# Part of a modulation's products moved to TensorE, its last two chunks singly, and another PSUM bank for what follows

## The chip, the cores and the metric

The kernel runs on one core of one Trainium2 chip. The metric is the device time of one execution in microseconds (us). Engines are named as the profile names them: PE is TensorE (its weight loads are PEld), DVE is VectorE, ACT is ScalarE, POOL is GpSimd, SP is SyncE, which issues most DMAs.

## The reference, cut to what matters

The program computes three transformer-like blocks on 512 tokens of width 1024. The change touches only the start of the first block. There the input `x` is modulated by a vector that comes from the conditioning input `c`, and the result is multiplied by a wide weight:

```python
mod = silu(c) @ w_ada + b_ada                 # w_ada: 1024 x 3072
shift, scale, gate = split(mod, 3)            # the first two are needed before anything else
h = x * (1 + scale) + shift                   # 512 x 1024
p = h @ w_in                                  # 1024 x 3712; the branches read slices of p
...
x = layer_norm(ALPHA * x + gate * o)          # the scaled x is kept until here
```

Everything is float32. For `h @ w_in` each float32 operand is split into a high and a low part and three products are added (high by high, high by low, low by high).

## The kernel before, in words

The width of 1024 is worked on in eight chunks of 128, numbered k = 0 to 7. The modulation phase (the `with self.ordered():` block in `block1`) streams `w_ada`, `x` and `w_in` from DRAM, and for each chunk does this:

1. Modulation: shift and scale of the chunk are dot products of silu(c) (tile `sc`, 128 x 8) with 128 columns of `w_ada`. `ada_acc` (called by `part`) lets ACT form the first of eight scaled terms and DVE add the other seven into the tile `acc`, a term for each 128 rows of `w_ada`. That leaves 128 partial sums a column, one for each partition; `sums` adds them on PE by a product of `acc` with a vector of ones, 128 x 1, and DVE adds the bias into `mod`.
2. `turned_x`: PE transposes the chunk of `x` by four 128 x 128 transposes.
3. `modulated`: ACT forms h from the transposed x with scale and shift, ACT rounds it to the high part (`aH`), DVE takes the low part (`aL`), and ACT writes the scaled x (`xa`, tiles named `res`).
4. `wsplit`: ACT and DVE split the chunk's row of `w_in` into `wh` and `wl`.
5. PE multiplies: 8 products with `aH` into four banks `psv`, 4 into two banks `psw` and `psk`, then 6 with `aL`.

Chunks are loaded in units (`UNITS`: first chunk, number of chunks): 0, 1, then pairs. A pair's modulation is found for both chunks at once; its accumulation is in two halves of 512 rows of `w_ada` (`part(cur, 0)`, `part(cur, 1)`). PE's order is fixed by a token, so a product stands where the source issues it: the `sums` of the next unit stand behind the eight `psv` products of a unit's last chunk, and the remaining ten products of that chunk behind them. DMAs are issued by SP in source order as well; the raw rows of `w_in` have three slots, so the load for chunk k waits for DVE's split of chunk k - 3.

After chunk 7, `psums` closes the banks and opens four new rings, which take up the eight banks in the order of its list. The first thing PE does then is `r_gemm(0)`, 24 products of 128 x 512 into the ring `po`, then `k_gemm(1)` into `mm`. Before, `po` is the last bank, the one in which `psk` lies; `psk` is read out by `shift_evac`, an ACT and a DVE instruction (`k<-sm,omu,sh`).

The lines that matter are short:

```python
def part(cur, q):
    ada_acc(cur[2], cur[1][q], range(4 * q, 4 * q + 4), 4 * q, self.act)
...
self.mm(pa[:, n * j + i : n * j + i + 1], cur[2][:, j, i * P : (i + 1) * P], self.ones[:, 0:1])
...
self.psums([("mm", 2), ("mg", 2), ("sm", 3), ("po", 1)])
```

Of the kernel before, what the change touches and what calls it, by code (L numbers as in the profile page):

```python
# [20 lines left out]
P = 128  # L21
T = 512
D = 1024
# [12 lines left out]
BEGUN = 1  # L36
LOW = 3
EARLY = 3
UNITS = ((0, 1), (1, 1), (2, 2), (4, 2), (6, 2))
TT = ("sm", "sm", "mm", "mm")  # L40
NFILL = 69
ORDER = "r0 A0 k1 g0 k2 r1 g0 n0 r2 f11 g0 f1 t0 g1 m0 g1 k3 g1 g2 l0 g2 r3 g3 l1 g2 f5 l2 f2 g3 l3 f3 l4 f2 g3 l5 f3 l6 f3 l7"
# [20 lines left out]
class Kern:  # L63
# [90 lines left out]
    def f(self, ap):  # L154
        return ap.bitcast(F32)
# [146 lines left out]
    def block1(self):  # L302
        nc, I, tc = self.nc, self.I, self.tc
        w_in, w_ada = I["w_in"], I["w_ada"]
# [9 lines left out]
        sc = b([P, 8], "sc")  # L314
# [8 lines left out]
        xaD = self.dp.tile([8, P, T], F32, tag="xaD", name="xaD")  # L323

        hH = [self.tl(self.ap_, [P, T], "aH", F32R) for _ in range(8)]
        hL = [self.tl(self.ap_, [P, T], "aL", F32R) for _ in range(8)]
# [14 lines left out]
        def ada_acc(acc, raw, steps, q0=0, first=None):  # L341

            for q in steps:
                if q == 0 and first:
                    first(acc, raw[:, q - q0], AF.Copy, scale=sc[:, q : q + 1])
                elif q == 0:
                    self.ts(acc, raw[:, q - q0], sc[:, q : q + 1])
                else:
                    self.stt(acc, raw[:, q - q0], sc[:, q : q + 1], acc, ALU.mult, ALU.add)
# [7 lines left out]
        xa = [self.tl(self.rp, [P, T], f"res{k}") for k in range(8)]  # L357

        def load(u):

            k0, n = UNITS[u]
            cs = slice(k0 * P, (k0 + n) * P)
            ada = []
            for q in range(n):
                raw = self.tl(sp, [P, 16 * P], "ada", bufs=5).rearrange("p (q j m) -> p q j m", j=2, m=n * P)
                r0, r1 = (0, D) if n == 1 else (512 * q, 512 * q + 512)
                for j in range(2):
                    src = w_ada[r0:r1, j * D + cs.start : j * D + cs.stop]
                    self.st(nc.sync.dma_start(out=raw[:, :, j, :], in_=src.rearrange("(k p) m -> p k m", p=P)))
                ada += [raw] if n == 2 else [raw[:, 0:4], raw[:, 4:8]]  # L370
                if q == 0:
                    xt = self.tl(sp, [P, NB, 2 * P], "xt", bufs=3)[:, :, : n * P]
                    self.st(nc.sync.dma_start(out=xt, in_=xv[:, :, cs]))
            return xt, ada, self.tl(sp, [P, 2, 2 * P], "acc")[:, :, : n * P]

        def wrows(k):
            ks = slice(k * P, (k + 1) * P)
            raw = self.wraw()
            rv = raw[:, : 6 * P].rearrange("p (k m) -> p k m", k=1)
            for o, c0, n in ((0, 512, T), (T, 3584, P), (T + P, 2048, P)):  # L380
                self.st(nc.sync.dma_start(out=rv[:, 0, o : o + n], in_=w_in[ks, c0 : c0 + n]))
            return rv

        def part(cur, q):
            ada_acc(cur[2], cur[1][q], range(4 * q, 4 * q + 4), 4 * q, self.act)

        def sums(u, cur):

            k0, n = UNITS[u]
            m2 = lambda z: z[:, 0:16].rearrange("p (j k) -> p j k", j=2)[:, :, k0 : k0 + n]  # L390
            pa = self.ptl("sm")
            for j in range(2):
                for i in range(n):
                    self.mm(pa[:, n * j + i : n * j + i + 1], cur[2][:, j, i * P : (i + 1) * P], self.ones[:, 0:1])
            self.tt(m2(mod), pa[:, 0 : 2 * n].rearrange("p (j k) -> p j k", j=2), m2(bada1), ALU.add)

        def turned_x(i, xt):
            ps = self.ptl("sm")
            for tb in range(NB):
                self.turn(ps[:, tb * P : (tb + 1) * P], xt[:, tb, i * P : (i + 1) * P])  # L400
            return ps
# [9 lines left out]
        with self.ordered():  # L411
            self.petoken = "start"
            cur = load(0)
            rv = wrows(0)
            pt = turned_x(0, cur[0])
            part(cur, 0)
            part(cur, 1)
            sums(0, cur)
            w_ = self.wsplit(rv, 1, 6 * P)
            modulated(0, pt)  # L420
            for k in range(8):
                wh, wl = w_
                u = [k in range(k0, k0 + n) for k0, n in UNITS].index(True)
                k0, n = UNITS[u]
                new, end = k == k0 and k0 + n < 8, k == k0 + n - 1
                if k < 7 and n == 2:
                    rv = wrows(k + 1)
                if new:
                    nxt = load(u + 1)
                if k < 7 and n == 1:  # L430
                    rv = wrows(k + 1)
                for f in loads[3 * k : 3 * k + 3]:
                    f()
                tok = [slice(tb * P, (tb + 1) * P) for tb in range(NB)]
                if new:
                    part(nxt, 0)
                    if n == 1:
                        part(nxt, 1)
                for tb in range(NB):
                    self.mm(psv[tb], hH[k][:, tok[tb]], wh[:, 0, :T], k == 0, False)  # L440
                    self.mm(psv[tb], hH[k][:, tok[tb]], wl[:, 0, :T], False, False)
                    if tb == (3 if end else 0) and k < 7:
                        pt = turned_x(0 if end else 1, (nxt if end else cur)[0])
                        if end:
                            sums(u + 1, nxt)
                            cur = nxt
                        w_ = self.wsplit(rv, 1, 6 * P)
                        modulated(k + 1, pt)
                        if new and n == 2:
                            part(nxt, 1)  # L450
                oz = ((T, psw), (T + P, psk))
                for o, pz in oz:
                    self.mm(pz, wh[:, 0, o : o + P], hH[k], k == 0, False)
                    self.mm(pz, wl[:, 0, o : o + P], hH[k], False, False)
                for tb in range(NB):
                    self.mm(psv[tb], hL[k][:, tok[tb]], wh[:, 0, :T], False, k == 7)
                for o, pz in oz:
                    self.mm(pz, wh[:, 0, o : o + P], hL[k], False, k == 7)
            self.petoken = None
            for k in range(8):  # L460
                self.st(nc.gpsimd.dma_start(out=xaD[k], in_=xa[k]))
        for _, turn in late:
            turn()
        sx.close()
# [142 lines left out]
        for tb in range(NB):  # L607
            vgs.append(a_([P, 8, 64], f"vn{tb}"))
            self.act(vgs[tb], psv[tb].rearrange("p (h i) -> p h i", i=64), AF.Gelu_apprx_tanh)
        self.psums([("mm", 2), ("mg", 2), ("sm", 3), ("po", 1)])  # L610

        def a_load():
            bsp = a_([P, 4, P], "bsp")
# [22 lines left out]
        def a_norm(tb):  # L636
            vg = vgs[tb]
            w = self.tl(av, [P, 8, 4], "lw", bufs=2)
            nc.vector.tensor_reduce(out=w[:, :, 0], in_=vg, axis=AX.X, op=ALU.add)
            self.ts(w[:, :, 0], w[:, :, 0], 1.0 / 64)  # L640
            self.tt(vg, vg, w[:, :, 0:1].to_broadcast([P, 8, 64]), ALU.subtract)
            sq = self.tl(av, [P, 8, 64], "gsq", bufs=1)
            self.act(sq, vg, AF.Square)
            nc.vector.tensor_reduce(out=w[:, :, 1], in_=sq, axis=AX.X, op=ALU.add)
            self.ts(w[:, :, 2], w[:, :, 1], 1.0 / 64, LN_EPS)
            self.pow_(w[:, :, 3], w[:, :, 2], -0.5)
            self.tt(vg, vg, w[:, :, 3:4].to_broadcast([P, 8, 64]), ALU.mult)
            return vg.rearrange("p h i -> p (h i)")
# [102 lines left out]
        for op, p in ORDER:  # L751
            if op == "r":
                r_gemm(p)
            elif op == "k":
                k_gemm(p)
            elif op == "g":
                go(p)
            elif op == "l":
                lmat(p // 2, p % 2)
            elif op == "f":  # L760
                fill(p)
            elif op == "A":
                bsp, wsp = a_load()
            elif op == "n":
                vn = [a_norm(tb) for tb in range(NB)]
            elif op == "t":
                wmT = a_turn(wsp, bsp)
            elif op == "m":
                for j in range(4):
                    a_mix(j, vn, bsp, wmT)  # L770
                a_free()
# [7 lines left out]
        r = lambda s, n, dt=F32: rp.tile(s, dt, tag=n, name=n)  # L779
# [226 lines left out]
        for c in range(NC_R):  # L1006
            late = [posts.pop(0) for _ in range(LATE[c])]
            steps = chain(c, between(c + 1, late))
            while True:
                with first():  # L1010
                    i = next(steps, None)
# [30 lines left out]
        o = Acts(oc)  # L1042
# [808 lines left out]
```

## Time and profile before

| | us |
|---|---|
| median of 3 runs (lowest to highest) | 1600.42 (1599.26 to 1603.02) |
| the profiled execution | 1600.12 |
| its span from first to last instruction | 1598.1 |
| PE busy in the span | 1531.5 (96%) |
| DVE busy | 915.0 (57%) |
| ACT busy | 722.9 (45%) |
| POOL busy | 256.7 (16%) |

All times inside the trace are counted from the span's start. The modulation phase takes the first 64.6 us. A float32 product that is not in the rounded form (the sums with ones, the transposes of other tiles) runs as two records on PE, so the trace counts two where the source has one. The granted clock (PEclk) is given as a share of 2.4 GHz: 1.00, or 0.50 for 1.2 GHz. Up to 18.4 us the trace holds no record of the clock and the column shows 1.00.

### The profile page before, as it was taken

How to read it: one execution, taken by the hardware profiler on the slowest of the kernel's cores; microseconds unless marked ns; L12 is line 12 of the kernel's file. 1: busy time of each engine (PE TensorE's matmuls, PEld its weight loads, DVE VectorE, ACT ScalarE, POOL GpSimd, SP SyncE). 2: the span in 40 equal slices, each digit the busy share in tenths (PEclk: the TensorE clock that was granted, in tenths of full speed). 3: DMA queues.
4: the chain of work that ended last, by engine and by line, in shares of the span. 5: the costliest groups of instructions: out<-in, count | busy, mean ns of one | idle time of the engine just before them, and what ended most of it. 6: DMA issues, size and time to landing. Idle time of an engine off the chain costs nothing.

```text
span 1598.1 us, 21745 instructions
## 1 busy us (share of the span) xinstructions
PE 1531.5 (96%) x8261; PEld 1298.2 (81%) x8261; DVE 915.0 (57%) x1621; ACT 722.9 (45%) x1318; POOL 256.7 (16%) x418
## 2 busy tenths in 40 slices
PE   5899989989999999999999999999999999999997
PEld 4787768889878899888888888888888988888886
DVE  6767677668767748233343456667755714343445
ACT  3545326646656556232232335667645524332231
POOL 3212110324300032000000033223323200000000
PEclk9999999999999999999999999999999999999999
DMA  9632556532233133333333232322213224232421
GB/s 312 190 104 85 104 150 174 171 109 77 60 79 86 41 93 93 94 102 94 93 94 104 79 106 60 109 70 76 71 53 106 93 66 120 81 103 66 132 79 53
DMA packets 260828, 161.16 MB, mean 101 GB/s; under 512 B 29553, under 2 KB 241124, under 8 KB 260724
## 3 DMA queue, kind: packets, MB, share of 16 engines
q1 hardware_dynamic: 258036, 153.40, 33.5%
q0 software_dynamic: 2544, 6.11, 1.3%
q8 instruction: 65, 1.06, 0.3%
q14 instruction: 39, 0.32, 0.1%
q10 hardware_dynamic: 144, 0.26, 0.0%
HBM read 146.90 MB, written 11.53 MB: 99 GB/s over the span
## 4 chain that ended last, share of the span: by engine, by line
PE 67%; DVE 5%; issue 2%; ACT 1%; DMA 1%; SPq 0%; POOL 0%; DVEq 0%; POOLq 0%; ACTq 0%
PE mm L144 58%; PE sm L144 4%; PE po L144 1%; PE sc L144 1%; DMA sw<-tr 1%; DVE bL L134 1%; DVE wl L124 1%; DVE res L124 1%; SPq L1320 0%; PE sm L150 0%; DVE mlom L134 0%; DVE hgmm L134 0%; PE pt L1380 0%; PE kv L144 0%; DVE mlpy L124 0%
## 5 line engine op out<-in xcount | busy, mean ns | idle before, releaser
L124 DVE TENSOR_TENSOR wl<-raw,wh 128x1024 fp32r<-128x1024 f32 (+3 forms) x244 | 287.1, 1178 | 294.4 <-ACT wh L141 290.3
L141 ACT CAST wh<-raw 128x1024 fp32r<-128x1024 f32 (+3 forms) x244 | 241.9, 994 | 459.6 <-PE mm L144 365.3
L144 PE MATMUL mm<-bL,wh 128*128 128x512 f32 (+1 forms) x752 | 280.3, 376 | 0.7 <-DVE bL L134 0.7
L144 PE MATMUL mm<-bH,wl 128*128 128x512 f32 (+1 forms) x752 | 279.7, 375 | 0.0
L144 PE MATMUL mm<-bH,wh 128*128 128x512 f32 (+1 forms) x752 | 278.3, 377 | 0.7 <-ACT t L138 0.7
L144 PE MATMUL mm<-aH,wh 128*128 128x512 f32 (+1 forms) x656 | 239.1, 366 | 5.0 <-ACT gsh L138 2.3
L144 PE MATMUL mm<-aL,wh 128*128 128x512 f32 (+1 forms) x656 | 236.7, 362 | 0.0
L144 PE MATMUL mm<-aH,wl 128*128 128x512 f32 (+1 forms) x656 | 236.2, 362 | 0.0
L144 PEld LDWEIGHTS mm<-bL,wh 128*128 128x128 f32 x752 | 140.7, 188 | 27.8 <-DVE bL L134 1.1
L144 PEld LDWEIGHTS mm<-bH,wl 128*128 128x128 f32 x752 | 140.8, 188 | 26.9
L144 PEld LDWEIGHTS mm<-bH,wh 128*128 128x128 f32 x752 | 139.0, 188 | 28.6 <-ACT t L138 1.1
L144 PEld LDWEIGHTS mm<-aH,wh 128*128 128x128 f32 x656 | 124.4, 190 | 26.0 <-ACT gsh L138 2.7
L144 PEld LDWEIGHTS mm<-aH,wl 128*128 128x128 f32 x656 | 124.6, 190 | 19.0 <-issue 0.2
L144 PEld LDWEIGHTS mm<-aL,wh 128*128 128x128 f32 x656 | 124.8, 190 | 17.7 <-issue 0.4
L144 PE MATMUL mm<-wh,aH 128*128 128x512 f32 x288 | 113.2, 395 | 1.7 <-ACT aH L141 1.7
L144 PE MATMUL mm<-wl,aH 128*128 128x512 f32 x288 | 112.9, 394 | 0.0
L144 PE MATMUL mm<-wh,aL 128*128 128x512 f32 x288 | 108.8, 393 | 0.0
L141 ACT CAST aH<-t 128x512 fp32r<-128x512 f32 (+1 forms) x74 | 40.9, 563 | 75.6 <-DVE t L124 75.5
L124 DVE TENSOR_TENSOR aL<-t,aH 128x512 fp32r<-128x512 f32 (+1 forms) x74 | 45.0, 617 | 36.8 <-ACT aH L141 36.8
L144 PEld LDWEIGHTS mm<-wh,aH 128*128 128x128 f32 x288 | 54.8, 190 | 13.0 <-ACT aH L141 1.8
L144 PEld LDWEIGHTS mm<-wl,aH 128*128 128x128 f32 x288 | 54.8, 190 | 11.4
L144 PEld LDWEIGHTS mm<-wh,aL 128*128 128x128 f32 x288 | 54.5, 190 | 11.6
(552 smaller groups left out, 2612.6 us busy)
## 6 DMA issues: line engine op xcount, KB each, us to landing
raw<-in_mlp_w_dram SPq DMA_DIRECT2D x128, 512.0 KB
raw<-in_hgrn_w_in_dram SPq DMA_DIRECT2D x32, 512.0 KB
raw<-in_w_in_dram SPq DMA_DIRECT2D x23, 512.0 KB
ada<-in_w_ada_dram SPq DMA_DIRECT2D x16, 512.0 KB
raw<-in_w_out_dram SPq DMA_DIRECT2D x10, 512.0 KB
raw<-in_w_ada_dram SPq DMA_DIRECT2D x8, 512.0 KB
raw<-in_mla_w_o_dram SPq DMA_DIRECT2D x8, 512.0 KB
raw<-in_hgrn_w_o_dram SPq DMA_DIRECT2D x8, 512.0 KB
```

The source lines that it names most:

```text
L124: self.st((eng or self.nc.vector).tensor_tensor(out=out, in0=a, in1=b, op=op))
L134: self.st(self.nc.vector.scalar_tensor_tensor(out=out, in0=a, scalar=s, in1=b, op0=op0, op1=op1))
L141: self.st(self.nc.scalar.copy(out=out, in_=in_))
L144: i = self.nc.tensor.matmul(out, l, r, start=start, stop=stop, **kw)
```

## The change

Five things change.

1. `direct(u)`: for unit 0 all eight terms of the modulation, and for the units of two chunks the second four, are no longer accumulated on DVE. `sums` multiplies the loaded blocks of `w_ada` (as weights) with the column of `sc` on PE and adds them in PSUM, behind the product of `acc` with ones where there is one. Unit 0 has 16 products instead of 2, the units of two chunks 20 instead of 4 each; DVE loses 7, 4 and 4 accumulations and ACT one.
2. `UNITS`: chunks 6 and 7 are units of their own. Each has 7 accumulations of 128 x 256 on DVE, and its own sums.
3. `load`: the units of one chunk, but for unit 0, load `w_ada` in four DMAs of 256 KB in place of two of 512 KB.
4. In a chunk, the two products of `aL` for `psw` and `psk` stand ahead of the four for `psv`.
5. `psums` lists `po` ahead of `sm`, so `po` is now the bank in which the parameter tile `pb` was transposed, and `psk`'s bank belongs to `sm`. The stores of `xa` to DRAM are issued in the source behind `a_norm` and without the token. In the built program they stand on POOL's queue where they stood before, one for one.

```diff
-UNITS = ((0, 1), (1, 1), (2, 2), (4, 2), (6, 2))
+UNITS = ((0, 1), (1, 1), (2, 2), (4, 2), (6, 1), (7, 1))
...
-                r0, r1 = (0, D) if n == 1 else (512 * q, 512 * q + 512)
...
+                rows = ((0, D),) if u == 0 else ((0, 512), (512, D)) if n == 1 else ((512 * q, 512 * q + 512),)
+                for r0, r1 in rows:
+                    q0 = 0 if n == 2 else r0 // P
...
-        def part(cur, q):
-            ada_acc(cur[2], cur[1][q], range(4 * q, 4 * q + 4), 4 * q, self.act)
+        def parts(u, cur):
+            for q in range(2):
+                if 4 * q not in direct(u):
+                    ada_acc(cur[2], cur[1][q], range(4 * q, 4 * q + 4), 4 * q, self.act)
+
+        def direct(u):
+
+            return range(8) if u == 0 else range(4, 8) if UNITS[u][1] == 2 else ()
...
-                    self.mm(pa[:, n * j + i : n * j + i + 1], cur[2][:, j, i * P : (i + 1) * P], self.ones[:, 0:1])
+                    m = slice(i * P, (i + 1) * P)
+                    steps = [(cur[2][:, j, m], self.ones[:, 0:1])] if u else []
+                    steps += [(cur[1][q // 4][:, q % 4, j, m], sc[:, q : q + 1]) for q in direct(u)]
+                    for o, (l, r) in enumerate(steps):
+                        self.mm(pa[:, n * j + i : n * j + i + 1], l, r, o == 0, o == len(steps) - 1)
...
+                for o, pz in oz:
+                    self.mm(pz, wh[:, 0, o : o + P], hL[k], False, k == 7)
                 for tb in range(NB):
                     self.mm(psv[tb], hL[k][:, tok[tb]], wh[:, 0, :T], False, k == 7)
-                for o, pz in oz:
-                    self.mm(pz, wh[:, 0, o : o + P], hL[k], False, k == 7)
             self.petoken = None
-            for k in range(8):
-                self.st(nc.gpsimd.dma_start(out=xaD[k], in_=xa[k]))
...
-        self.psums([("mm", 2), ("mg", 2), ("sm", 3), ("po", 1)])
+        self.psums([("mm", 2), ("mg", 2), ("po", 1), ("sm", 3)])
```

On PE the program begins, before, with the transposes of chunk 0 (`xt`), the two products of `acc` with ones, and then the first products of `h`:

```order
L150 MATMUL sm_179<-ident,xt_172 128x128 x4
L144 MATMUL sm_192<-ones,acc_174 128x1 x2
L144 MATMUL mm_153<-wh_196,aH_122 128x512
L144 MATMUL mm_153<-wl_197,aH_122 128x512
L144 MATMUL mm_154<-wh_196,aH_122 128x512
```

In the changed program the same place reads:

```order
L150 MATMUL sm_179<-ident,xt_172 128x128 x4
L144 MATMUL sm_184<-sc,ada_169 128x1 x16
L144 MATMUL mm_153<-wh_202,aH_122 128x512
L144 MATMUL mm_153<-wl_203,aH_122 128x512
L144 MATMUL mm_154<-wh_202,aH_122 128x512
```

Sixteen products on the loaded `w_ada` itself stand where two on the accumulated tile stood, ahead of every product of `h`.

On PE at the end of chunk 1's `psv` products, before, the transposes of chunk 2 and the four sums of unit 2 (chunks 2 and 3) stand ahead of chunk 1's other products:

```order
L150 MATMUL sm_294<-ident,xt_265 128x128 x4
L144 MATMUL sm_299<-ones,acc_270 128x1 x4
L144 MATMUL sm_157<-aH_123,wh_243 128x512
L144 MATMUL sm_157<-aH_123,wl_244 128x512
L144 MATMUL sm_158<-aH_123,wh_243 128x512
```

In the changed program:

```order
L150 MATMUL sm_298<-ident,xt_273 128x128 x4
L144 MATMUL sm_303<-ones,acc_278 128x1
L144 MATMUL sm_303<-sc,ada_275 128x1 x4
L144 MATMUL sm_303<-ones,acc_278 128x1
L144 MATMUL sm_303<-sc,ada_275 128x1 x4
L144 MATMUL sm_303<-ones,acc_278 128x1
L144 MATMUL sm_303<-sc,ada_275 128x1 x4
L144 MATMUL sm_303<-ones,acc_278 128x1
L144 MATMUL sm_303<-sc,ada_275 128x1 x4
L144 MATMUL sm_157<-aH_123,wh_251 128x512
```

Twenty sums stand there now, each group opened by one that needs DVE's `acc`; the same row stands at the end of chunk 3 for unit 3.

On DVE around chunk 7 of the changed program (`aL_136` is chunk 6's low part, `aL_137` chunk 7's, `wl_592` chunk 7's weight and `wl_713` that of `r_gemm(0)`):

```order
L124 TENSOR_TENSOR aL_136<-h_95_539,aH_128 128x512
L134 SCALAR_TENSOR_TENSOR acc_561<-ada_554,sc,acc_561 128x2x128 x7
L124 TENSOR_TENSOR mod<-sm_587,bada_111 128x2
L124 TENSOR_TENSOR wl_592<-raw_562,wh_591 128x768
L124 TENSOR_TENSOR wl_713<-raw_710,wh_712 128x1024
L124 TENSOR_TENSOR aL_137<-h_104_595,aH_129 128x512
```

Before, it reads:

```order
L124 TENSOR_TENSOR aL_136<-h_96_510,aH_128 128x512
L124 TENSOR_TENSOR wl_537<-raw_525,wh_536 128x768
L124 TENSOR_TENSOR wl_672<-raw_669,wh_671 128x1024
L124 TENSOR_TENSOR aL_137<-h_101_540,aH_129 128x512
L294 COPY pb<-sm_587 128x69
```

An accumulation of seven and a `mod` now stand between chunk 6's low part and chunk 7's weight.

## Rows read from the trace of the kernel before

**Rows 1.** The page's first line.
```profile
span 1598.1 us, 21745 instructions
```
**Rows 2.** Stretches: busy time and records of each engine, granted clock, DMA share.
```profile
core 0: us, PE busy (x) PEld busy (x) DVE busy (x) ACT busy (x) POOL busy (x), PEclk, DMA share, GB/s
...
24.50:28.30 3.80, 0.02 (x1) 0.05 (x1) 3.49 (x5) 0.83 (x1) 0.00 (x0) 1.00 1.08 361
...
29.60:35.50 5.90, 5.90 (x17) 4.63 (x18) 4.72 (x7) 3.22 (x5) 0.55 (x1) 0.50 1.10 351
35.50:64.60 29.10, 28.58 (x142) 23.36 (x140) 19.50 (x33) 17.14 (x26) 7.25 (x18) 1.00 0.81 250
64.60:69.30 4.70, 0.05 (x1) 0.00 (x0) 4.70 (x10) 4.09 (x8) 0.72 (x3) 1.00 1.06 257
69.30:73.10 3.80, 3.75 (x9) 2.93 (x10) 2.55 (x4) 0.63 (x1) 1.81 (x2) 0.55 0.73 192
73.10:120.00 46.90, 46.66 (x272) 37.96 (x271) 30.71 (x48) 21.26 (x32) 9.61 (x6) 1.00 0.29 90
...
148.20:155.00 6.80, 5.91 (x17) 4.59 (x17) 4.95 (x9) 2.94 (x5) 3.27 (x3) 0.50 0.44 116
```
**Rows 3.** Timeline, chunks 0 and 1: start, duration, engine, line, operation [idle before <-releaser].
```profile
8.57 1.12 PE L150 MATMUL sm<-ident,xt 128*128 128x128 f32 x4 [5.35 <-DMA xt<-in_x_dram]
...
11.93 1.02 PE L144 MATMUL sm<-ones,acc 128*128 128x1 f32 x4 [2.24 <-DVE acc L134]
...
12.38 0.57 PE L144 MATMUL sm<-ones,acc 128*128 128x1 f32 x2
...
12.98 0.16 DVE L124 TENSOR_TENSOR mod<-sm,bada 128x2 f32<-128x2 f32 x1 [1.11 <-PE sm L144]
...
14.66 0.80 PE L144 MATMUL mm<-wh,aH 128*128 128x512 f32 x1 [1.71 <-ACT aH L141]
...
15.53 3.65 DVE L134 SCALAR_TENSOR_TENSOR acc<-ada,sc,acc 128x256 f32<-128x256 f32 x7 [0.20 <-ACT acc L138]
...
19.24 0.61 PE L144 MATMUL sm<-ones,acc 128*128 128x1 f32 x4 [0.28 <-DVE acc L134]
```
**Rows 4.** Timeline, the sums of unit 2 and the first product of chunk 2.
```profile
22.66 5.48 DVE L134 SCALAR_TENSOR_TENSOR acc<-ada,sc,acc 128x512 f32<-128x512 f32 x7 [0.41 <-ACT acc L138]
...
28.28 1.44 PE L144 MATMUL sm<-ones,acc 128*128 128x1 f32 x8 [3.78 <-DVE acc L134]
...
33.99 0.63 PE L144 MATMUL mm<-wh,aH 128*128 128x512 f32 x1
```
**Rows 5.** Timeline, the last unit's second half on DVE and its sums on PE.
```profile
49.03 3.11 DVE L134 SCALAR_TENSOR_TENSOR acc<-ada,sc,acc 128x512 f32<-128x512 f32 x4
...
52.28 1.02 PE L144 MATMUL sm<-ones,acc 128*128 128x1 f32 x8 [0.52 <-DVE acc L134]
...
52.28 0.91 PE L144 MATMUL sm<-ones,acc 128*128 128x1 f32 x7 [0.52 <-DVE acc L134]
```
**Rows 6.** What engines waited for ahead of instructions on `acc`: us in total, times.
```profile
  DMA ada<-in_w_ada_dram: 4.0, 1
```
**Rows 7.** Timeline, the first products behind the phase, on PE, and what releases them.
```profile
68.56 0.74 DVE L134 SCALAR_TENSOR_TENSOR k<-sm,omu,sh 128x512 f32<-128x512 f32 x1
...
69.35 0.53 PE L144 MATMUL po<-aH,wh 128*128 128x512 f32 x1 [4.70 <-DVE k L134]
...
73.10 0.39 PE L144 MATMUL po<-aH,wh 128*128 128x512 f32 x1
...
76.55 0.39 PE L144 MATMUL mm<-aH,wh 128*128 128x512 f32 x1
```
**Rows 8.** Timeline of PE ahead of a later fall of the clock.
```profile
144.71 0.95 PE L144 MATMUL po<-ind,cum 128*128 128x2 f32 x8
145.59 1.16 PE L144 MATMUL sm<-AR,BK 64*128 64x128 f32 x8
149.09 2.07 PE L144 MATMUL sm<-AR,BK 64*128 64x128 f32 x8 [2.34 <-ACT res L141]
```

More of the change, by code (lines that the diff above doesn't have):

```diff
@@ L365, in load @@
                 raw = self.tl(sp, [P, 16 * P], "ada", bufs=5).rearrange("p (q j m) -> p q j m", j=2, m=n * P)
-                r0, r1 = (0, D) if n == 1 else (512 * q, 512 * q + 512)
-                for j in range(2):
-                    src = w_ada[r0:r1, j * D + cs.start : j * D + cs.stop]
-                    self.st(nc.sync.dma_start(out=raw[:, :, j, :], in_=src.rearrange("(k p) m -> p k m", p=P)))
+                rows = ((0, D),) if u == 0 else ((0, 512), (512, D)) if n == 1 else ((512 * q, 512 * q + 512),)
+                for r0, r1 in rows:
+                    q0 = 0 if n == 2 else r0 // P
+                    for j in range(2):
+                        src = w_ada[r0:r1, j * D + cs.start : j * D + cs.stop]
+                        dst = raw[:, q0 : q0 + (r1 - r0) // P, j, :]
+                        self.st(nc.sync.dma_start(out=dst, in_=src.rearrange("(k p) m -> p k m", p=P)))
                 ada += [raw] if n == 2 else [raw[:, 0:4], raw[:, 4:8]]
@@ L415, in block1 @@
             pt = turned_x(0, cur[0])
-            part(cur, 0)
-            part(cur, 1)
             sums(0, cur)
@@ L434, in block1 @@
                 tok = [slice(tb * P, (tb + 1) * P) for tb in range(NB)]
[L435 to L438, printed above, removed]
+                if new and n == 1:
+                    parts(u + 1, nxt)
                 for tb in range(NB):
@@ L449, in block1 @@
                         if new and n == 2:
-                            part(nxt, 1)
+                            parts(u + 1, nxt)
                 oz = ((T, psw), (T + P, psk))
@@ L765, in block1 @@
                 vn = [a_norm(tb) for tb in range(NB)]
+                for k in range(8):
+                    nc.gpsimd.dma_start(out=xaD[k], in_=xa[k])
             elif op == "t":
```

## The prediction

> **What bounds the kernel now.** I read the page first, then the table of stretches, then the timeline of the first 80 us, then the view of the tile `acc`. The reader is to see three things.
>
> PE sets the end of the modulation phase and of what follows. From 35.5 to 64.6 it is busy 28.58 of 29.10 us, from 73.1 to 120 it is busy 46.66 of 46.90 [rows 2]. So what is added to PE's work there is paid in full, and only PE's idle stretches can be won back.
>
> There are three of these worth naming: 2.24 us before the first sums, which wait for DVE's accumulation [rows 3]; 3.78 us before the sums of unit 2, for the same reason [rows 4]; and 4.70 us after the phase, when the first `po` product waits until DVE has read `psk` out of the same bank, at 68.56 + 0.74 [rows 7].
>
> The clock makes two of them dearer. Behind the second and the third idle stretch the granted clock is 0.50 (29.60 to 35.50, and most of 69.30 to 73.10) [rows 2]. Nine `po` products take 69.35 to 73.10, 0.42 us each; the next fifteen take 73.10 to 76.55, 0.23 each [rows 7].
>
> w_ada's transfers are no bound: over the whole phase an engine sat idle for them once, 4.0 us before the first accumulation [rows 6].
>
> **The change part by part.** First the price of a sum. A 128 x 1 product is two records. At 1.00 seven records take 0.91 us and eight 1.02 [rows 5], so a record is 0.11. In the first burst the last two of four start 0.45 after the first (12.38 against 11.93) [rows 3], so there a record is 0.22; that is the lower clock, whatever the column shows so early.
>
> (a) Unit 0. The accumulation goes (2.24 us of PE's wait), but PE gets 32 records for 4. They can start when the four transposes are through, at about 9.5 (8.57 + 1.12, less the 0.2 by which products overlap) [rows 3]. At 0.22 they end at 9.5 + 7.0 + 0.2 = 16.7; before, the sums ended at 12.95. Loss 3.7 us. Were they to run at 0.11 they would end at 13.2, a loss of 0.2. I take 3.7: the engine has done nothing but four transposes, and the four sums at this place did run at 0.22.
>
> Chunk 1 hangs on the same chain: from `mod` at 12.98 to its sums at 19.24 it is 6.3 us of h, high part, scaled x and DVE's 3.65 [rows 3], which the change leaves alone. So it comes 3.7 later too, and PE reaches the sums of unit 2 at 24.50 + 3.7 = 28.2 [rows 2].
>
> (b) Unit 2. DVE now has three of the seven accumulations, 5.48 x 3/7 = 2.35, and is done at 22.66 + 3.7 + 2.35 = 28.7 [rows 4]. The sums start at 28.8, against 28.28: the idle time that the edit removes has been spent by (a). There are 40 records for 8. At 0.11 they end at 33.3, against 29.72. The ten products between them and chunk 2 took 29.72 to 33.99 at the lower clock, 4.3 us; at 1.00 they take 2.3, so chunk 2 begins at 35.6, 1.6 late, and saves another 0.7 because before it ran at 0.50 until 35.50. Loss by chunk 2's end 0.9, if the clock holds.
>
> (c) Unit 3. Before, these sums did not wait [no idle between 35.5 and 64.6 beyond 0.52, rows 2, 5]. 32 more records at 0.11: 3.5 us.
>
> (d) Units 4 and 5, chunks 6 and 7 singly. The first has 4 records for 8 (gain 0.45) and its seven accumulations, 3.65, are ready about 0.4 sooner than the half that was waited for 0.52 [rows 3, 5]: gain 0.8. The second has 4 records (loss 0.45), and its chain from `mod` is again 6.3 us, for which PE has 18 products of 0.23 and four transposes at half of the first ones' 1.12, 4.7 us. PE waits 1.6. Loss 2.1. The smaller pieces of w_ada are hidden: they were not waited for, and PE is later than before. Without that cover the four extra issues on SP would cost up to their own time; SP's next load waits for a slot of raw weights anyway.
>
> (e) The bank. `po` waits for the read of `pb`, made while chunk 7 multiplies. So the 4.70 us go, and with them the fall of the clock behind: 9 x (0.42 - 0.23) = 1.7. Gain 6.4. What is late next is the weight of `k_gemm(1)`, a row that DVE does before the phase ends, and then nothing for 24 products each. The stretch from 73.1 shows that DVE is busy 30.71 of 46.90 us, so it can follow when PE is 6.4 nearer.
>
> (f) Two `aL` products earlier: same products, other order, 0. The stores of scaled x: same places on POOL's queue, 0 from both sides.
>
> (g) The clock in the bursts. This is the only unknown of size. Two bursts, (b) and (c), last 4.4 us each and hold nothing but 128 x 1 products. No burst before is longer than 1.44. The nearest rows speak against their holding the clock. At 28.28 PE began with 1.44 us of sums, went on with dense products, and got no higher clock until 35.50, 7.2 us; at 69.35 it began with dense products and had it after 3.75 [rows 2, 4, 7]. And at 148.2 the clock fell behind 2.0 us of small products (eight of 128 x 2, eight on half the rows) and 2.34 of idling [rows 8], less idle time than in the other cases. So I take it that the clock falls behind a burst of sums as it did behind idling, and that each burst brings one stretch at 0.50 like those at 29.6 (5.9 us and more) and 148.2 (6.8 us) [rows 2]. 6.8 us at half the clock are 3.4 us lost. Bounds for each: 0, and 3.4.
>
> The Trainium skill, TensorE: Matmul & The Clock Gate, section "Why this matters for your kernels", blames idle gaps between bursts of matmuls for the loss of the clock. By that rule two bursts in which PE is never idle would keep 1.00, and the sum would be 6.8 us lower; rows 8 agree with it only in part.
>
> Sum for the phase: (a, b) 0.9, (c) 3.5, (d) -0.8 + 2.1, together 5.7; with two falls 12.5. Less 6.4 for the bank: 6.1 us slower. The profiled execution is 1600.12 (span 1598.1 [rows 1] and 2.0 around it), which is 0.3 under the median. 1606.2, and I say 1606. Behind 120 us every engine's order is the one before, so I let the shift run through to the end.
>
> **The rivals.**
>
> Only one burst costs the clock (the other straddles dense work on both sides): 6.1 - 3.4 = 2.7, 1602.8. For it: falls came at differing delays after the work stopped. Against it: both bursts are three times the longest seen.
>
> The clock holds in both: 6.1 - 6.8 = -0.7, 1599.4. For it: PE is never idle. Against it: the two places named in (g).
>
> The other side, faster: sums keep the clock as dense products do, and it rises in the first burst already. At 69.35 it rose 3.75 us after PE began; counted from the transposes at 8.57 it would rise at 12.3. By then 13 records are done, the other 19 take 2.1, and the sums end at 14.6, 1.6 late instead of 3.7. With the clock held later, -0.7 - 2.1 = -2.8, 1597.3. It decides where a stretch of sums at 9.5 goes from 0.22 to 0.11 a record. Against it: the stretch from 28.28, where sums and dense products together did not raise the clock for 7.2 us. With bounds of 0.2 in (a) it reaches 1596.
>
> A loss further on: PE comes 6.4 us nearer to DVE and ACT behind the phase, meets a wait there, and the bank's gain goes: up to 12.5, 1612. Against it: DVE's and ACT's idle time from 73.1 to 120 (16 and 26 us) [rows 2].
>
> That the change does not do what it says holds for the stores alone, and costs nothing.
>
> **How the numbers follow.** Two falls 0.48 (its own range 1603.5 to 1609: falls of 2.7 to 4.5 each as they come early or late in a burst, and (a) at 3.0 to 3.7), one fall 0.12, the clock holds 0.16, it rises early 0.19, a loss further on 0.05. The range reaches from 1596.5, the early rise's lower part, to 1609.5; outside are the dearest case and the edges. A measurement here can tell about 0.2%, 3.2 us. Slower by more: 0.45 + 0.04 + 0.05 = 0.54. Within: 0.03 of the first, 0.08, 0.14 and 0.05: 0.30. Faster by more, below 1597.2: 0.02 of the third and 0.14 of the fourth, 0.16.
>
> **What would show it.** In the changed profile: 32 sum records from about 9.5, at 0.22 each, and `mod` near 16.7; sums of unit 2 from about 28.8, with a clock of 0.50 during or behind them and records that go from 0.11 to 0.22 on the way; the same behind chunk 3; a wait of about 1.6 us for `acc` before the sums of chunk 7; the phase's end near 77 rather than 64.6; and the first `po` product right behind it, without idle time and at 0.23 us. If the clock stays at 1.00 from 20 to 77, or the first burst speeds up on its way, the forecast is wrong by the terms given. If the first `po` product still waits, (e) is wrong.

## The result, and the profile after

Five runs of the changed kernel have the median 1612.95 us (1608.11 to 1614.86), five of the kernel before 1599.81. The ratio is 1.0071 (95% interval 1.0059 to 1.0083): 11.4 us slower, 9 to 13 by the interval. The forecast was 1606, its range ended at 1609.5. The direction came true, the size did not.

The profiled execution took 1611.48, its span is 1609.2 for 1598.1 [rows 1]: 11.1 more. Three stretches add up to that. They meet at two places that both traces have: the start of the first `po` product less its wait, which I call the phase end, and the second group of the small products `po<-ind,cum` (128 x 2; eight records a group), which stands about 50 us behind it.

| stretch | before | after | difference | forecast |
|---|---|---|---|---|
| start to phase end | 64.65 | 78.51 | +13.9 | +12.5 |
| phase end to second group of `ind` | 52.62 | 50.05 | -2.6 | -6.4 |
| from there to the end of the span | 1480.8 | 1480.6 | -0.2 | 0 |

The first step came as forecast. Timeline of PE and DVE in the changed kernel (start, duration, engine, line, operation, count, [idle before <- releaser]):

```profile
9.40 6.83 PE L144 MATMUL sm<-sc,ada 128*128 128x1 f32 x32
...
16.26 0.16 DVE L124 TENSOR_TENSOR mod<-sm,bada 128x2 f32<-128x2 f32 x1 [12.02 <-PE sm L144]
...
28.77 0.35 PE L144 MATMUL sm<-ones,acc 128*128 128x1 f32 x2 [0.63 <-DVE acc L134]
28.98 1.03 PE L144 MATMUL sm<-sc,ada 128*128 128x1 f32 x8
...
30.10 1.83 PE L144 MATMUL sm<-sc,ada 128*128 128x1 f32 x8
...
36.06 0.77 PE L144 MATMUL sm<-aH,wh 128*128 128x512 f32 x1
```

The 32 records of unit 0 run at 0.21 each and `mod` is there at 16.26 for 12.98 [rows 3]. Unit 2's records begin at 28.77 (forecast 28.8); eight take 1.03, and from 30.10 on eight take 1.83: the price nearly doubles in the middle of the burst, as term (g) said. The stretches show the clock (us, busy time and records of PE, PEld, DVE, ACT, POOL, granted clock, DMA share, GB/s):

```profile
30.13:40.37 10.24, 10.24 (x39) 9.37 (x40) 2.77 (x4) 2.61 (x4) 0.55 (x1) 0.50 0.59 192
40.37:50.61 10.24, 10.24 (x66) 9.03 (x66) 2.95 (x4) 3.23 (x5) 0.54 (x1) 1.00 1.10 310
50.61:57.44 6.83, 6.83 (x23) 5.77 (x23) 2.77 (x4) 2.61 (x4) 0.54 (x1) 0.50 0.53 146
57.44:78.50 21.06, 19.18 (x94) 15.59 (x93) 14.44 (x31) 10.88 (x17) 4.96 (x13) 1.00 0.43 125
78.50:102.90 24.40, 24.34 (x109) 19.03 (x107) 20.43 (x35) 17.73 (x27) 8.27 (x11) 1.00 0.62 153
102.90:104.62 1.72, 0.00 (x1) 0.00 (x1) 1.72 (x5) 1.00 (x2) 0.00 (x0) 1.00 0.07 19
104.62:108.64 4.02, 4.02 (x11) 3.15 (x12) 2.48 (x5) 0.00 (x0) 3.85 (x2) 0.58 0.78 216
```

In the first and the third row PE is busy all the time, and the clock is 0.50: two falls, one for each burst, at 1.2 of 2.4 GHz. Ahead of the first burst PE stood 0.63 for DVE; in e2 below, both falls come without any such wait. The last two rows are what the forecast did not have. PE works almost without a gap from the phase's end to 102.90 (24.34 of 24.40 us), stands for 1.72, and goes on at half clock from 105.2 to 108.6. The chain behind that wait, in the timeline of all engines:

```profile
78.51 0.40 PE L144 MATMUL po<-aH,wh 128*128 128x512 f32 x1
...
80.42 0.38 SPq L624 DMA_DIRECT2D wsp<-in_w_spatial_dram  x1
...
88.21 1.09 POOL L625 TENSOR_SCALAR_AFFINE_SELECT wsp<-wsp 128x1024 f32<-128x1024 f32 x1 [7.18 <-DMA wsp<-in_w_spatial_dram]
89.28 3.32 POOL L246 TENSOR_TENSOR lw<-lw,pwm 128x8 f32<-128x8 f32 x2
...
90.99 0.69 DVE L124 TENSOR_TENSOR vn<-vn,lw 128x512 f32<-128x512 f32 x1 [2.28 <-POOL lw L246]
...
103.82 0.74 DVE L134 SCALAR_TENSOR_TENSOR k<-mm,omu,sh 128x512 f32<-128x512 f32 x1
...
104.62 0.50 PE L144 MATMUL mm<-aH,wh 128*128 128x512 f32 x1 [1.72 <-DVE k L134]
```

Read it from below. PE waits for a bank of `mm` that DVE has yet to read; it does so at 103.82 (`k_gemm`'s shift). DVE is late, since from 90.99 on it does row after row without idling and before that it stood 2.28 us for POOL. POOL makes the powers of `a_norm` (`lw<-lw,pwm`), and these stand in its queue behind the masking of `w_spatial`, which waits 7.18 us for its load. The first `po` product, with 4.70 of wait in [rows 7], has none any more. The same chain lies in the kernel before, under PE's wait and its half clock, where it cost nothing (timeline of the kernel before):

```profile
71.29 1.09 POOL L618 TENSOR_SCALAR_AFFINE_SELECT wsp<-wsp 128x1024 f32<-128x1024 f32 x1 [5.52 <-DMA wsp<-in_w_spatial_dram]
...
74.07 0.69 DVE L124 TENSOR_TENSOR vn<-vn,lw 128x512 f32<-128x512 f32 x1 [1.66 <-POOL lw L246]
...
92.08 0.74 DVE L134 SCALAR_TENSOR_TENSOR k<-mm,omu,sh 128x512 f32<-128x512 f32 x1
...
94.99 0.48 PE L144 MATMUL mm<-aH,wh 128*128 128x512 f32 x1
```

DVE was through at 92.82 and PE came at 94.99: a slack of 2.2 us. In the changed kernel, counted from the phase end, PE would have come to this place at 24.4 us for 30.3, 6.0 sooner, and DVE was through at 26.1 for 28.2, 2.1 sooner. 6.0 less the slack and less what DVE gained is 1.7, the wait that the trace shows. With half of the 3.4 us at half clock behind it that makes 3.4 of the 3.8 us that are missing in the table.

### The profile page after: what moved, and what is told of

Its sections match the earlier page's. It is cut to its first block, busy times and chain, and to the rows that moved or that the text cites. A ratio compares the mean times of both kernels' runs of the same rounds, so it can differ in the third digit from the quotient of the medians.

```text
span 1609.2 us, 21933 instructions
## 1 busy us (share of the span) xinstructions
PE 1551.3 (96%) x8353; PEld 1317.8 (82%) x8353; DVE 908.0 (56%) x1614; ACT 723.1 (45%) x1318; POOL 255.9 (16%) x418
## 4 chain that ended last, share of the span: by engine, by line
PE 69%; DVE 4%; issue 2%; ACT 1%; POOL 1%; DMA 0%; SPq 0%; DVEq 0%; POOLq 0%; ACTq 0%
PE mm L144 59%; PE sm L144 5%; PE po L144 2%; PE sc L144 1%; DVE bL L134 1%; DVE res L124 1%; DVE wl L124 1%; PE pt L1389 0%; PE sm L150 0%; DVE hgmm L134 0%; DVE mlom L134 0%; PE kv L144 0%; DVE mlpy L124 0%; PE po L150 0%; DVE mlpy L134 0%
## 5 line engine op out<-in xcount | busy, mean ns | idle before, releaser
L144 PEld LDWEIGHTS mm<-wh,aL 128*128 128x128 f32 x288 | 55.2, 192 | 11.8
```

Of the source, the lines that this page charges most:

```text
L144: i = self.nc.tensor.matmul(out, l, r, start=start, stop=stop, **kw)
```

## The experiments

Two theories stood against each other for the missing 3.8 us. P: POOL's wait for `w_spatial`, by the chain above. D: DVE simply has too much to do behind the phase. A third question was what the products on TensorE cost, and whether their bursts cost the clock. Each row below is one kernel: the ratio to the kernel before, then from its profile the phase end, how long after it POOL began to mask `w_spatial`, what PE then waited for DVE behind the phase, and the time from the phase end to the second `ind` group. The ratio comes from 6 to 12 runs (5 of the changed kernel), the other columns from one execution. A difference of two ratios carries both intervals, about 0.2% or 3 us either way.

| kernel | ratio (95%) | phase end | masking | PE's wait | to `ind` |
|---|---|---|---|---|---|
| before | 1 | 64.65 | +6.6 | 4.70 at `po` | 52.6 |
| changed | 1.0071 (1.0059 to 1.0083) | 78.51 | +9.7 | 1.72 | 50.1 |
| e1, before with the bank | 0.9982 (0.9970 to 0.9994) | 64.04 | +7.9 | 2.52 | 50.6 |
| e10, before with the `aL` order | 0.9982 (0.9971 to 0.9994) | 62.94 | +6.9 | 1.12 at `po` | 47.4 |
| e2, changed without the bank | 1.0044 (1.0027 to 1.0061) | 76.43 | +9.1 | 1.12 at `po`, 0.37 | 47.9 |
| e3, changed without products on PE | 0.9976 (0.9964 to 0.9988) | 65.81 | +7.7 | 1.06 | 49.0 |
| e4, of these unit 0 only | 1.0004 (0.9994 to 1.0014) | 69.20 | +7.0 | 0 | 46.2 |
| e6, unit 3 only, one burst | 1.0030 (1.0019 to 1.0041) | 69.10 | +9.4 | 1.72 | 49.7 |
| e9, unit 3 only, spread | 1.0012 (1.0001 to 1.0023) | 67.53 | +9.7 | 1.68 | 50.0 |
| e8, e3 with pairs | 0.9951 (0.9935 to 0.9966) | 62.99 | +7.1 | 0 | 46.2 |
| e5, changed, `w_spatial` early | 1.0033 (1.0022 to 1.0045) | 76.44 | -29.5 | 0 | 46.4 |
| e7, e8 with `w_spatial` early | 0.9957 (0.9942 to 0.9972) | 65.07 | -17.4 | 0 | 46.4 |
| e12, e8 with a dose of products | 0.9974 (0.9963 to 0.9985) | 61.77 | +8.0 | 1.39 | 47.8 |
| e14, e12 with `w_spatial` early | 0.9952 (0.9938 to 0.9967) | 62.67 | -14.2 | 0 | 46.3 |

### The bank and the order of aL: e1, e2, e10

e1 is the kernel before with one line changed, e2 the changed kernel with it undone:

```diff
-        self.psums([("mm", 2), ("mg", 2), ("sm", 3), ("po", 1)])
+        self.psums([("mm", 2), ("mg", 2), ("po", 1), ("sm", 3)])
```

> The kernel before with the bank change alone; every engine's order is the one before. Theory A (the gain of 6.4 us read from the first po products runs through to the end): 1599.8 - 6.4 = 1593.4. Theory B (behind the phase the norm rows on DVE and the powers on POOL keep their pace, PE reaches a bank that DVE has not yet read, waits there and drops to the clock of 0.50, as at 102.9 to 108.6 in the changed kernel, 1.7 us of wait and 1.7 us of half clock): 1593.4 + 3 to 4 = 1596.5 to 1597.5, with a wait of PE for DVE's k between 90 and 100 us and a stretch at 0.50 behind it.

> The changed kernel with the old order of banks. Theory A: the wait for the read of psk comes back ahead of the first po product, 1613 + 6.4 = 1619.4. Theory B: that wait gives DVE and POOL their time back and the later wait (1.7 us, and 1.7 at half clock) goes, so 1613 + 6.4 - 3.6 = 1616. A third reading: the two aL products moved ahead already let DVE read psk earlier, so the wait is shorter than 4.7 us and the time is below 1615.

e10 is the kernel before with the `aL` products of `psw` and `psk` ahead of those of `psv`:

```diff
+                for o, pz in oz:
+                    self.mm(pz, wh[:, 0, o : o + P], hL[k], False, k == 7)
                 for tb in range(NB):
                     self.mm(psv[tb], hL[k][:, tok[tb]], wh[:, 0, :T], False, k == 7)
-                for o, pz in oz:
-                    self.mm(pz, wh[:, 0, o : o + P], hL[k], False, k == 7)
```

> The kernel before with the two aL products of psw and psk moved ahead of psv's, nothing else. Term (f) says 0: 1600. The trace of the changed kernel without the bank change shows the first po product waiting 1.1 us instead of 4.7 and no stretch at 0.50 behind it, and the norms' rows on DVE and ACT standing later in their queues: by that 1600 - 3.6 - 1.7 = 1595, and the bank has only the last 1.1 us to give, so that bank and order together (1593.8) are little better than this.

The bank alone gains 2.9 us (1 to 5) and not 6.4. Every engine's order is the one before in e1, so this is the bank's effect undisturbed, and its timeline shows the gain being taken back, on the same chain (POOL, DVE, DVE, PE):

```profile
71.91 1.09 POOL L618 TENSOR_SCALAR_AFFINE_SELECT wsp<-wsp 128x1024 f32<-128x1024 f32 x1 [6.52 <-DMA wsp<-in_w_spatial_dram]
...
74.69 0.69 DVE L124 TENSOR_TENSOR vn<-vn,lw 128x512 f32<-128x512 f32 x1 [3.60 <-POOL lw L246]
...
83.56 0.75 DVE L134 SCALAR_TENSOR_TENSOR k<-mm,omu,sh 128x512 f32<-128x512 f32 x1
...
84.36 0.50 PE L144 MATMUL mm<-aH,wh 128*128 128x512 f32 x1 [2.52 <-DVE k L134]
```

DVE's wait for POOL has grown from 1.66 to 3.60, and PE waits 2.52, at the bank before the one at which it waits in the changed kernel. Theory A of the expectation falls. B holds, though the wait came at 84 and not between 90 and 100. The profiled execution of e1 was the slowest of its twelve: behind the second `ind` group it took 1485.9 us for 1480.8 before, with 40 us at half clock for 27. So its profile shows the chain, and the size of the gain is taken from all the runs.

The order of `aL` alone gains 2.9 us too (1 to 5), and term (f) had it at nothing. With `psw` and `psk` finished four products sooner, their read-outs run while PE still multiplies, and in e10's timeline the first `po` product waits 1.12 in place of 4.70, with the clock at 1.00 behind it:

```profile
64.06 0.50 PE L144 MATMUL po<-aH,wh 128*128 128x512 f32 x1 [1.12 <-DVE k L134]
```

5 us were expected of e10, and 2.9 arrive at the end. In its profile the second `ind` group comes 6.9 us sooner than before, and 4.9 of these are lost again behind it, with 37 us at half clock for 27. The kernel with both bank and order, e8 below, is 0.31% faster than e10 (2 to 8 us), though its `ind` group comes only 1.2 sooner. Why e10 keeps so little stays open.

In the changed kernel, which has this order, the bank thus had 1.1 us left to give, as the third reading for e2 has it. Even this was not worth it there: without the bank the changed kernel is faster by 0.27% (1 to 8 us). After the short wait at `po` PE waits 0.37 for 1.72 further on, with no fall of the clock. Part of the difference is the phase, which in e2's profile ended 2.1 sooner with the same instructions in it; how much I can't separate.

### POOL's wait: e5, e7

e5 issues the load of `w_spatial` with those of chunk 4 (into a tile of its own), so that POOL masks it long before the phase ends; e7 does the same to e8:

```diff
+                if k == 4:
+                    self.st(nc.sync.dma_start(out=wsp, in_=I["w_spatial"].rearrange("g t s -> t g s")))
...
-            wsp = a_([P, 8, P], "wsp")
-            nc.sync.dma_start(out=wsp, in_=I["w_spatial"].rearrange("g t s -> t g s"))
```

> The changed kernel with the load of w_spatial issued in chunk 4 of the modulation phase and its masking on POOL there; else as changed (DVE's norm rows move a few places). Theory P (behind the phase POOL waits for that load with the powers of the norms behind it; DVE's multiplication waits for the powers, and the read of the bank stands behind that on DVE): DVE's wait of 2.3 us at 88.7 goes, so does PE's of 1.7 us at 102.9 and the 1.7 us of half clock behind it: 3.4 us faster than the changed kernel, 1609.5. Theory D (DVE simply has too much to do there): PE still waits for DVE's k and the time stays at 1613.

> The kernel of pairs with the early load of w_spatial. Theory P: the wait behind the phase goes and the whole 6.4 us of the bank's term stays, 1593.5. Theory D: as the kernel of pairs.

The changed kernel becomes 0.38% faster, about 6 us (3 to 9); P asked for 3.4. In e5's timeline (POOL, DVE, DVE, PE) POOL waits for DVE now and no longer the other way, and PE has no wait for DVE from 76.44 to the second `ind` group, 46.4 us later for 50.1:

```profile
83.47 4.02 POOL L246 TENSOR_TENSOR lw<-lw,pwm 128x8 f32<-128x8 f32 x2 [3.58 <-DVE lw L131]
...
86.56 0.68 DVE L124 TENSOR_TENSOR vn<-vn,lw 128x512 f32<-128x512 f32 x1
...
99.68 0.74 DVE L134 SCALAR_TENSOR_TENSOR k<-mm,omu,sh 128x512 f32<-128x512 f32 x1
...
100.47 0.50 PE L144 MATMUL mm<-aH,wh 128*128 128x512 f32 x1
```

In the profiles 3.7 us are that stretch, and the phase ended 2.1 sooner here too. (This execution was the slowest of e5's ten and lost 3.8 again behind the `ind` group; the ratio is taken from all of them.) D falls as the cause: DVE has the same rows to do and is in time. But only just: its read ends at 100.42 and PE's product begins at 100.47, so a larger gain would have met DVE again. e7 changes nothing against e8, because e8's masking begins at +7.1 and DVE does not wait for it.

The table tells how close it is, among the kernels with both bank and `aL` order changed: with the masking at +7.0 or +7.1 PE has no wait, at +7.7 1.06, at +8.0 1.39, from +9.4 on 1.7. What makes the load land sooner or later is not shown; it is issued 0.3 to 1.9 us behind the phase end in these kernels, soonest in e12, which masks late. e3 and e4 have the same order behind the phase, and only the landing differs. In e3's timeline of DVE the multiplication by the powers stands 11.5 behind the phase end, after a wait for POOL, and PE then waits 1.06:

```profile
77.28 0.69 DVE L124 TENSOR_TENSOR vn<-vn,lw 128x512 f32<-128x512 f32 x1 [0.92 <-POOL lw L246]
```

In e4's it stands 10.1 behind, without a wait, and PE has none:

```profile
79.32 0.68 DVE L124 TENSOR_TENSOR vn<-vn,lw 128x512 f32<-128x512 f32 x1
```

### The products on TensorE and the clock: e3, e4, e6, e9

e3 returns `()` from `direct` and accumulates as before; e4 returns `range(8)` for unit 0 alone, e6 `range(4, 8)` for unit 3 alone, on e3. e9 has e6's sixteen products, but one each behind ten dense products of chunk 2 and six of chunk 3 (`one` issues the next of them; one of the places):

```diff
                     self.mm(psv[tb], hH[k][:, tok[tb]], wh[:, 0, :T], k == 0, False)
+                    if end and tb < 3:
+                        one(todo)
```

> The changed kernel with all sums of the modulation made from DVE's accumulated tile, as before; last two chunks singly, bank, order of aL and stores as changed. My terms for the products on TensorE come to (a, b) 0.9, (c) 3.5 and two falls of 3.4, 11.2 together; the trace after shows the phase end at 78.5 for 64.7, 13.9, of which 1.3 are the single chunks'. So 1613 - 12 = 1601 if the products are the whole loss of the phase; 1597 or less if the shorter phase also takes away the later wait for DVE.

> As the kernel without products on TensorE, but with those of unit 0. Term (a) says 3.7 us more than that kernel, of which up to 2 may be won back at unit 2, whose sums then wait less for DVE... the idle time before them is 3.8 us in the kernel before and the accumulation that sets it starts 3.7 later too, so nothing is won back: + 3.7. Theory of an early rise of the clock: + 1.6. The difference between this kernel and the changed one is then the price of units 2 and 3 (bursts and clock): 8 us by the terms.

> The kernel without products on TensorE, but with those of unit 3 alone: 32 more records in one burst, 3.5 us at 0.11 each. Nothing waits there, so the accumulations saved on DVE win nothing. If the burst costs the clock: 3.5 + 3.4 = 6.9 us more than that kernel, with a stretch at 0.50 beginning in the burst (from about 40.2 to 45). If it keeps the clock: 3.5 more.

> The kernel without products on TensorE, but with those of unit 3, one each between the dense products of chunks 2 and 3 (as groups of their own, added to the sums of acc by one row more on DVE) instead of in one burst. 32 more records cost 3.5 us as in the kernel with the burst. If it is the burst that costs the clock, no stretch at 0.50 begins between 40 and 50 us, and the phase ends 1.7 us sooner than with the burst (69.1), at 67.4. If it is the share of records that do not count, the clock falls all the same: 69 or more.

All products together cost 0.95%, 15 us between e3 and the changed kernel, for 12 expected; in the profiles the phase is 12.7 of it. Unit 0's cost 0.28% (4.5 us; the phase ends 3.4 later; (a) said 3.7), the rest 0.67% (11 us for 8 expected; in the profiles the phase is 9.3 longer, and the stretch behind it, where e4 has no wait for DVE, 3.9).

e6 and e9 settle the clock at unit 3. In e6 the burst stands from 39.92 to 44.4, PE is never idle, and the clock falls in it (stretches, columns as above):

```profile
39.90:44.60 4.70, 4.70 (x43) 4.70 (x42) 0.00 (x0) 0.00 (x0) 0.00 (x0) 0.95 1.12 327
44.60:47.60 3.00, 3.00 (x8) 2.32 (x9) 2.24 (x4) 2.75 (x5) 0.54 (x1) 0.50 0.96 238
```

In e9's stretches the same records lie between dense products, and it stays at 1.00:

```profile
35.50:44.40 8.90, 8.90 (x63) 8.14 (x62) 0.69 (x1) 1.24 (x3) 0.54 (x1) 1.00 1.12 319
44.40:47.60 3.20, 3.20 (x17) 2.63 (x18) 2.35 (x5) 2.69 (x5) 0.51 (x1) 1.00 0.99 242
```

The phase ends at 67.53 for 69.10, to a tenth what was expected, and the ratio is 0.18% lower, about as much as two ratios can tell. e2 adds that no wait is needed ahead of a burst: there PE has none from 17.8 to 62.1, and the clock is 0.50 from 34.0 to 37.4 and from 47.7 to 54.5, each fall near the end of a burst or in it. The rule of the Trainium skill that the prediction weighed (TensorE: Matmul & The Clock Gate, "Why this matters for your kernels": idle gaps between bursts of matmuls lose the clock) does not hold alone here: a burst of 128 x 1 products without a gap loses it as well.

Of e6 only half was expected rightly: the phase ends 3.3 later than e3's, as 3.5 of records say, and the fall in the burst seems to cost nothing more: e3 has a fall of its own behind PE's wait for chunk 7, which e6 lacks. But the ratios are 0.54% apart, 8.6 us. In the profiles 3.3 of their 7.0 us are the phase, 0.7 the stretch behind it, by the later masking, and 3.0 lie behind the second `ind` group, where e6 has more time at half clock (33 us for 23); why it falls there stays open.

### Pairs, and a dose in the waiting time: e8, e12, e14

e8 is e3 with `UNITS` ending in `(6, 2)` again. e12 moves two of eight terms to PE at units 0 and 2 only, ahead of the sums of `acc`:

```diff
-            return ()
+            return (6, 7) if u in (0, 2) else ()
```

> The kernel without products on TensorE, with the chunks 6 and 7 as a pair again: the kernel before with the bank, the order of aL and the stores changed. Singles cost 2.1 - 0.8 = 1.3 us by term (d): 1.3 less than the kernel with them, 1595.5. If the order of aL does nothing, as (f) says, it is equal to the kernel before with the bank alone, 1598.5.

> The kernel of pairs without the other products on TensorE, but with two of the eight products at units 0 and 2, placed ahead of the sums of acc, in the time in which PE waits for DVE there (2.2 us at either place); DVE has two multiplications fewer at either. Unit 0: DVE is done 2 x 0.52 us sooner, less one row of 0.16 more behind the sums; 8 records at 0.22 lie in the wait. Unit 2: DVE is done 2 x 0.78 sooner; 16 records at 0.11 lie in the wait. Gain 0.9 + 1.3 = 2.2 us if PE waits for DVE only: 1591.6. If the clock falls for it, 1.7 of that goes.

> The kernel of the dose (two of eight products at units 0 and 2, pairs, bank and aL order changed) with the early load of w_spatial. With the load late, its phase ended at 61.77 (62.99 without the dose), and PE then waited 1.39 us for DVE's k, which waits for POOL. Theory P: that wait goes, the stretch from the first po product to the second group of ind is 46.3 us for 47.8, and the phase keeps its 1.2 us: 1.5 us less than the dose alone and about 1.2 less than the kernel of pairs, 1592.5 to 1595. Theory D: as the dose alone, 1596.5.

The single chunks cost 0.25%, 4 us (1 to 7), for 1.3 by term (d). The wait was there as forecast (1.69 in e3). What the term lacked was the half clock that follows it in e3's stretches, and e3's later masking, by which PE waits 1.06 behind the phase and e8 does not:

```profile
57.50:60.90 3.40, 3.40 (x9) 2.75 (x10) 2.86 (x4) 1.89 (x3) 0.70 (x3) 0.50 0.17 33
```

The dose lies in PE's wait as meant, and shortens it from 2.16 in e8 (e12's timeline of PE, unit 2):

```profile
23.60 1.84 PE L144 MATMUL sm<-sc,ada 128*128 128x1 f32 x16
...
25.87 1.05 PE L144 MATMUL sm<-ones,acc 128*128 128x1 f32 x8 [0.43 <-DVE acc L134]
```

The phase ends at 61.77 for 62.99, 1.2 sooner and not 2.2: at the sums of unit 3 PE now waits 1.05 for DVE, where e8 has no wait. And e12 is not faster than e8 but 0.23% slower (1 to 7 us). `w_spatial` is late again (+8.0), PE waits 1.39, and the stretch behind the phase is 1.6 longer. That makes only 0.4 us of the loss; the rest is not in the profiles, where e12's span is 0.5 shorter than e8's. With the load early (e14) the wait is gone, and the ratio is e8's. The dose's own gain is below what these runs can tell. The best of all kernels are e8, e7 and e14, 0.43 to 0.49% faster than the kernel before (7 to 8 us), 1.1 to 1.2% faster than the changed one.

## Why the prediction was wrong

- **What bounds.** Right: PE's added work was paid in full, 13.9 us by the phase end in this execution; e2 and e5, with the same phase, show 11.8. The 12.5 of the sum lie between.
- **(a), (b), (c).** Right: 0.21 a record in unit 0, sums of unit 2 from 28.77, 0.11 going to 0.23. e4 against e3 gives 3.4 for (a).
- **(g).** Right in kind, two falls: e6 and e9 show it for unit 3, e2 for both bursts. The first lasted 10.2 instead of 6.8, which is 1.7 us of the 13.9.
- **(d).** The wait came (1.66 before the sums of chunk 7). In the changed kernel no fall follows it; in e3 and e4 one does, and there the term is too small.
- **(f).** Wrong. "Same products, other order, 0": the order of `aL` alone gains 2.9 us (e10) and cuts the wait at `po` from 4.70 to 1.12. It does a large part of what (e) put down to the bank. The stores stand on POOL's queue in both traces between the same instructions; no run moves them alone.
- **(e), the failed step.** The 4.70 and the half clock went as forecast. But "it can follow when PE is 6.4 nearer" was read from DVE's idle share, and the shift did not "run through": of the 6.4, 3.8 did not come, 3.4 of them by 1.72 of wait and the half clock behind it. The rival "a loss further on" named that very event, and got 0.05, because DVE and ACT had 16 and 26 us of idle time there. Idle time in a stretch is no slack at one instruction. The slack was 2.2 us, and the rows at 71.29 and 74.07, which the prediction did not look at, showed who would use it up: a load, then POOL, then DVE. The 6.4 themselves were sized rightly: with the load early (e5), or landing sooner than in the changed kernel (e8), the stretch takes 46.4 and 46.2 us for 52.6. e1 shows the loss with the bank alone (2.9 us for 6.4), e5 its cause.

With (e) at 2.6 the same sum gives 1600.1 + 12.5 - 2.6 = 1610; the profiled execution took 1611.5, and the 1.4 between them are the phase.

## What to carry to other kernels

Before a wait of the bounding engine is booked as gain, look at the next buffers that it will ask for, and take for each the time between its release and its use: beyond the smallest of these the gain depends on whether the releasing engine can come sooner at that very instruction, however idle it is on average. Look through the waits that other engines have under the wait to be removed, above all a queue that holds an instruction on a late load ahead of short work that others need. Small products that must go to PE are better put between dense ones than into a burst (e9 against e6); put into time in which PE waits, they won nothing that these runs can tell (e12, e14).

## What the runs showed of the hardware that was not expected

Sixteen f32 products of 128 x 1 (32 records), with four sums in one burst, cost the clock with PE busy throughout (4.70 of 4.70 us in e6, both bursts in e2); the same sixteen, each behind a dense product, did not (e9: 1.00 from 35.5 to 47.6). When the clock falls, and for how long, is not fixed by the instructions: the same phase held 17.1 us at 0.50 in the changed kernel, 10.2 in e2 and 13.7 in e5, and ended at 78.51, 76.43 and 76.44.
